# Wide products of the gate and up blocks in groups of four, the first corner's bank read out early, operands in one piece

## The chip, the cores and the metric

One core of a Trainium2 chip runs the whole program. Engines are named as in the profile: PE multiplies matrices, PEld loads its weights, DVE and ACT work on whole tiles, POOL and SP issue transfers here. The metric is the device time of one execution in microseconds (us), lower is better; three executions of the kernel before took 1763.86 to 1764.58, median 1764.16.

## The reference

Two layers; each runs three token mixers side by side, merges them, and then a feed-forward block and a gated input embedding. The change lies in the feed-forward block and in the normalisation ahead of it.

```python
for i in range(DEPTH):                      # DEPTH = 2, S = 512 tokens, D = 1024
    ...                                     # mixers, merge
    x = x + merged @ w_o[i]
    h = rmsnorm(x, norm_ffn[i])
    x = x + (jax.nn.silu(h @ w_ffn_gate[i]) * (h @ w_ffn_up[i])) @ w_ffn_down[i]   # 1024 -> 2816 -> 1024
    h = rmsnorm(x, norm_ple[i])
    x = x + jax.nn.sigmoid(h @ w_ple_gate[i]) * (p[i] @ w_ple_in[i])
```

## The kernel before

All data is float32, and every product is made of three float32r products: each operand is split into a high part and a low remainder (`split` for weights, `operand` for activations), and high x high, high x low and low x high are summed. ACT makes the high part of a weight tile, DVE the low one. Activations lie transposed, 128 channels in the partitions and 512 tokens in a row, so one PSUM bank (512 float32 in a row) holds one block of 128 outputs for all tokens.

The feed-forward block (`ffn`) goes through 22 blocks of 128 hidden units, in three parts of 8, 7 and 7, and after each part multiplies by its share of the down weights (L1141 to L1147). A block needs gate and up weights against all of h. `seven` does this with seven products in place of eight, Winograd's way on a 2x2 split: its weights are a11, a12, a22 and the sums s1 to s4 (two transfers add up weights as they land, DVE does the other sums), its activations the quarters b11, b21, b22 and their differences t1 to t4, made once for the layer in `quarters`. Each product sums over four pieces of 128 channels, for one half (256) of the tokens.

Blocks with an even number are narrow: per piece three matmuls of 256 columns (L1011 to L1013), high weights on high and low activations, then low weights on high activations. Blocks with an odd number are wide (`twice`): high and low activations stand next to each other as 512 columns, so one matmul of 512 columns (L1008) does the first two, into two halves of the bank, and one of 256 (L1009) does the third; the two halves are added afterwards on ACT and DVE. T (s1 x t3) is narrow in every block, so an odd block has six wide products.

A block uses three banks, C, A and Q, and one of the two `tr` banks for T. Even blocks take C, A, Q from the three `mm` banks, odd blocks from the two `sc` and the one `av`. C gets a11 x b11; ACT copies it to A (L1023); A gets s3 x t2, and ACT copies that to Q (L1037); C gets a12 x b21 (`corner`), which completes the gate's first half; A gets s2 x t1 and is copied out (L1043, L1044, or L1046 in a narrow block); Q gets a22 x t4 and gives the up halves; A gets s4 x b22 (L1061), which completes the gate's second half. In a wide block C and A are both read out after that last product (L1063 to L1065). The next block of the same kind can't write C before C's sum has been read, nor copy into A before A's has.

Two blocks run interleaved: `sevens_of` steps the generators, so that block n+1 does its step (a) (C and its copy), block n its (d) (s2 and a22), n+1 its (b) (T), n its (e) (s4), n+1 its (c) (s3, corner). The order on PE is that of the code. On DVE, ACT and the queues a scheduler orders by priority; the weights' loads, sums and splits run ahead with raised priority, and `behind` pins one instruction behind another on the same engine. ACT and DVE work strictly in the order that the scheduler made. The split of s3 and s4 goes into one of two fixed pairs of tiles (`spare`): `pt` for even blocks, `y` for odd ones. `held`, `mark` and `cleared` are marks for `behind`.

In the normalisation ahead of it (`w_o`, `norm_chunk`), the tile of h has its high half in columns 0 to 511 and its low half behind it. For even chunks of channels only the first 256 tokens are made, for odd ones all 512. So high and low of the same 256 tokens, the operand of a wide matmul, are two runs of 256, with a gap of 256 between them.

Of the kernel before, what the change touches and what calls it, by code (L numbers as in the profile page):

```python
# [20 lines left out]
P = 128  # L21
# [40 lines left out]
class Net:  # L62
# [212 lines left out]

    def norm_chunk(self, k, x, g, tag, st, n=512):

        if k == KD - 1:
            self.sumsq(k, x, st)
        if n < 512:  # L280
            tag = self.sb(tag, [P, 2, 512], F32R)[:, :, :n]
        h = self.operand(x[:, :n], g, tag)
        if k < KD - 1:
            self.sumsq(k, x, st)
        return h
# [675 lines left out]
    def seven(self, wg, wu, bs, tags, spare, md, first, fb, early, twice):  # L961


        nc = self.nc
        with self.tc.high_priority(offset=min(self.w_ahead, self.tc.cur_priority - self.p0)):
# [30 lines left out]
            self.tt(s4, s3, g[:, up], ALU.add)  # L996
            halve(*spare, sums[1], ("s3", "s4"))
        shape = (P, 2, 256) if twice else (P, 256)
        C, A, Q = (self.ps(t, shape) for t in tags)

        def product(out, w, b, first=False):
            wh, wl = ws[w]
            mm = nc.tensor.matmul
            for k in range(4):
                c = slice(k * P, k * P + P)
                both = bs[k][b]
                if len(out.shape) > 2:
                    mm(out, wh[:, c], both, start=first and k == 0, stop=False, skip_group_check=True)  # L1008
                    mm(out[:, 0], wl[:, c], both[:, 0], start=False, stop=k == 3, skip_group_check=True)  # L1009
                    continue  # L1010
                mm(out, wh[:, c], both[:, 0], start=first and k == 0, stop=False, skip_group_check=True)  # L1011
# [30 lines left out]
        if twice:  # L1042
            self.act(uu[:, 1], A[:, 0], AF.Copy)  # L1043
            self.cleared = self.act(gg[:, 0], A[:, 1], AF.Copy)  # L1044
        else:
            self.cleared = self.act(uu[:, 1], A, AF.Copy)  # L1046
        product(Q, "a22", "t4")
        if twice:
            self.tt(uu[:, 1], uu[:, 1], gg[:, 0], ALU.add)
            self.act(uu[:, 0], Q[:, 1], AF.Copy)  # L1050
            self.tt(uu[:, 0], Q[:, 0], uu[:, 0], ALU.add)
            self.tt(uu, uu, gg[:, 1:2].to_broadcast([P, 2, 256]), ALU.add)
        else:
# [68 lines left out]
    def ffn(self, h, x):  # L1122
# [5 lines left out]
        md8 = [self.sb(t, [P, 2, 512], F32R) for t in ["v"] * 3 + ["z"] + ["y"] * 3]  # L1128
        md8.append(tuple(self.sb("e", [P, 512], F32R) for _ in range(2)))
        self.sums, self.sevens = [t for _ in range(2) for t in self.parts_of("qk", [1024], 2)], 0  # L1130
        for part in PARTS:
            mids = md8[:len(part)]
            self.sevens_of((self.seven(self.a["w_fg"][i, fb], self.a["w_fu"][i, fb], bs,
                                       (("mm", "mm", "mm"), ("sc", "sc", "av"))[fb % 2],
                                       spare[fb % 2], md8[f], part[0] and f < 2, fb, fb == 0,
                                       fb % 2 == 1)
                            for f, fb in enumerate(part)), part[0] == 0)
# [368 lines left out]
```

## Time and profile before

| | |
|---|---|
| median of three executions | 1764.16 us (1763.86 to 1764.58) |
| the profiled execution, whole | 1764.9 us |
| its span, first to last instruction | 1763.1 us |
| granted PE clock, mean | 0.999 |
| DVE / ACT busy | 79% / 53% of the span |

The span is what the trace shows, and 1.8 us of the profiled execution lie outside it. Rows of the timeline have the start in us, the duration, the engine, the source line, and what is written from what; in square brackets stands the idle time before it and what ended it. A matmul's duration includes the way through the array, so neighbours overlap: what a matmul costs in a run of matmuls is the distance from its start to the next one's.

### The profile page before, as it was taken

Reading aid. Unit: us, or ns where it says so; the run is one execution under the profiler, and the core shown is the slowest. Engines: PE = TensorE matmul, PEld = TensorE weight load, DVE = VectorE, ACT = ScalarE, POOL = GpSimd, SP = SyncE. Lnnn points to the kernel's source line nnn. Section 1 sums busy time; section 2 is a strip of 40 time slices with the busy share of each in tenths; the row PEclk is TensorE's granted clock in tenths of the full one; section 3 lists DMA queues with packets and bytes.
Section 4 is the critical chain, followed back from the end, with each engine's and each line's share of the span. In section 5 each row is a group of like instructions: output and inputs, shape, how many; then the busy total and the mean of one; then the engine's idle time right before and its main releaser. Section 6 shows DMA issues by size and latency. Waiting matters only on the chain.

```text
span 1763.1 us, 26202 instructions
## 1 busy us (share of the span) xinstructions
PE 1756.3 (100%) x9618; PEld 1525.2 (87%) x9618; DVE 1388.2 (79%) x2264; ACT 934.6 (53%) x1649; POOL 104.1 (6%) x114
## 2 busy tenths in 40 slices
PE   9999999999999999999999999999999999999998
PEld 7889888888899898898888888888888998989987
DVE  7967988998788676777776789889887875877776
ACT  5566555326576264464545655552356653645554
POOL 0000000000121020100000000000001210201000
PEclk9999999999999999999999999999999999999999
DMA  6565641334767365543445655322356664656332
GB/s 227 163 188 157 164 123 54 102 99 150 223 161 181 119 170 154 141 118 131 149 137 166 190 148 153 111 75 93 101 182 190 180 166 122 177 143 154 97 105 96
DMA packets 114785, 253.90 MB, mean 144 GB/s; under 512 B 16864, under 2 KB 23776, under 8 KB 114656
## 3 DMA queue, kind: packets, MB, share of 16 engines
q1 hardware_dynamic: 101264, 227.83, 41.9%
q0 software_dynamic: 12672, 23.07, 8.0%
q8 instruction: 76, 1.25, 0.3%
q10 hardware_dynamic: 720, 1.31, 0.2%
q14 instruction: 53, 0.43, 0.1%
HBM read 215.46 MB, written 7.34 MB: 126 GB/s over the span
## 4 chain that ended last, share of the span: by engine, by line
PE 99%; DVE 0%; ACT 0%; POOL 0%; issue 0%; POOLq 0%; ACTq 0%; DVEq 0%
PE ffn_sc L1008 6%; PE ffn_mm L179 4%; PE ffn_mm L180 4%; PE ffn_mm L181 4%; PE ffn_mm L1011 4%; PE ffn_mm L1013 4%; PE ffn_mm L1012 4%; PE ffn_sc L1009 3%; PE mergea_mm L179 2%; PE mergea_mm L181 2%; PE mergea_mm L180 2%; PE diff_sc L798 2%; PE diff_mm L179 2%; PE diff_mm L180 2%; PE gatec_mm L180 2%; PE natten_mm L180 2%
## 5 line engine op out<-in xcount | busy, mean ns | idle before, releaser
L160 DVE SCALAR_TENSOR_TENSOR conv_z<-glu_z,pre_par,conv_z 128x512 f32<-128x512 f32 x240 | 179.4, 748 | 3.4
L143 ACT ACTIVATE ffn_wh<-ffn_wr 128x1024 fp32r<-128x1024 f32 (+1 forms) x92 | 92.6, 1020 | 117.1 <-PE ffn_mm L180 61.4
L157 DVE TENSOR_TENSOR ffn_wl<-ffn_wr,ffn_wh 128x1024 fp32r<-128x1024 f32 (+1 forms) x92 | 107.1, 1175 | 40.2 <-ACT ffn_wh L143 39.7
L976 POOL DMA_DIRECT2D ffn_qk<-w_fu x88 | 78.0, 974 | 595.6 <-DMA ffn_qk<-w_fu 308.0
L157 DVE TENSOR_TENSOR ffn_t<-ffn_mm,wo_rb 128x512 f32<-128x512 f32 (+1 forms) x86 | 47.9, 557 | 55.1 <-PE ffn_mm L181 46.9
L143 ACT ACTIVATE mergea_wh<-mergea_wr 128x1024 fp32r<-128x1024 f32 (+1 forms) x32 | 27.1, 846 | 96.8 <-PE mergea_mm L180 79.5
L157 DVE TENSOR_TENSOR ffn_t<-ffn_t,ffn_t 128x512 f32<-128x512 f32 x88 | 54.4, 619 | 18.0 <-ACT ffn_t L143 18.0
L157 DVE TENSOR_TENSOR ffn_wl<-ffn_qk,ffn_wh 128x1024 fp32r<-128x1024 f32 x44 | 53.8, 1223 | 16.6 <-ACT ffn_wh L143 16.6
L1008 PE MATMUL ffn_sc<-wo_h,ffn_wh 128*128 128x512 f32 x176 | 64.2, 399 | 0.1
L143 ACT ACTIVATE ffn_wh<-ffn_qk 128x1024 fp32r<-128x1024 f32 x44 | 46.6, 1060 | 31.4 <-PE ffn_mm L180 16.2
L143 ACT ACTIVATE diff_a<-diff_sc,diff_s 128x512 f32<-128x512 f32 x32 | 22.1, 689 | 70.8 <-DVE diff_s L891 70.8
L181 PE MATMUL ffn_mm<-ffn_v,ffn_wl 128*128 128x512 f32 x132 | 51.4, 390 | 0.0
L180 PE MATMUL ffn_mm<-ffn_v,ffn_wh 128*128 128x512 f32 x132 | 51.4, 390 | 0.0
L179 PE MATMUL ffn_mm<-ffn_v,ffn_wh 128*128 128x512 f32 x132 | 51.3, 389 | 0.0
L179 PE MATMUL ffn_mm<-ffn_y,ffn_wh 128*128 128x512 f32 x132 | 51.3, 389 | 0.0
L180 PE MATMUL ffn_mm<-ffn_y,ffn_wh 128*128 128x512 f32 x132 | 51.3, 389 | 0.0
L181 PE MATMUL ffn_mm<-ffn_y,ffn_wl 128*128 128x512 f32 x132 | 51.3, 389 | 0.0
L1011 PE MATMUL ffn_mm<-wo_h,ffn_wh 128*128 128x256 f32 x176 | 50.0, 284 | 0.0
L1012 PE MATMUL ffn_mm<-wo_h,ffn_wh 128*128 128x256 f32 x176 | 49.8, 283 | 0.0
L1013 PE MATMUL ffn_mm<-wo_h,ffn_wl 128*128 128x256 f32 x176 | 49.8, 283 | 0.0
L1009 PE MATMUL ffn_sc<-wo_h,ffn_wl 128*128 128x256 f32 x176 | 49.5, 281 | 0.0
L143 ACT ACTIVATE natten_wh<-natten_wr 128x1024 fp32r<-128x1024 f32 x24 | 25.4, 1058 | 42.1 <-issue 15.2
(847 smaller groups left out, 6325.4 us busy)
## 6 DMA issues: line engine op xcount, KB each, us to landing
ffn_qk<-w_fu POOLq DMA_DIRECT2D x88, 256.0 KB, 6.3
ffn_wr<-w_fg SPq DMA_DIRECT2D x44, 512.0 KB, 4.4
ffn_wr<-w_fd SPq DMA_DIRECT2D x32, 448.0 KB, 4.0
ffn_r<-w_fu SPq DMA_DIRECT2D x44, 256.0 KB, 3.3
ffn_qk<-w_fg SPq DMA_DIRECT2D x44, 256.0 KB, 3.2
ffn_qk<-w_fu SPq DMA_DIRECT2D x44, 256.0 KB, 3.4
natten_wr<-w_in SPq DMA_DIRECT2D x16, 512.0 KB, 4.0
diff_wr<-w_in SPq DMA_DIRECT2D x16, 512.0 KB, 4.2
```

The costliest lines, as they stand in the source:

```text
L143: i = self.nc.scalar.activation(out, in_, func, **kw)
L157: return self.nc.vector.tensor_tensor(out, a, b, op)
L160: return self.nc.vector.scalar_tensor_tensor(out, a, s, b, op0, op1)
L179: mm(out, wh, ah, start=first, stop=False, **kw)
L180: mm(out, wh, al, start=False, stop=False, **kw)
L181: mm(out, wl, ah, start=False, stop=last, **kw)
L976: nc.gpsimd.dma_start(q, wu[:, lo], accum_op=ALU.add)
L1008: mm(out, wh[:, c], both, start=first and k == 0, stop=False, skip_group_check=True)
L1009: mm(out[:, 0], wl[:, c], both[:, 0], start=False, stop=k == 3, skip_group_check=True)
L1011: mm(out, wh[:, c], both[:, 0], start=first and k == 0, stop=False, skip_group_check=True)
L1012: mm(out, wh[:, c], both[:, 1], start=False, stop=False, skip_group_check=True)
L1013: mm(out, wl[:, c], both[:, 0], start=False, stop=k == 3, skip_group_check=True)
```

## The change

Four things are edited.

1. In a wide product the four matmuls of 512 columns come first, one for each piece, and then the four of 256 columns; before they took turns.
2. In a wide block, the corner's sum is read out of C right behind the corner's product (an ACT copy of the second half, a DVE add of the first) into `gg[:, 0]`. What was parked in `gg` until then (T's copy and half of A's) goes to a tile of its own, `side`, of which there are two, taken from tag `e`.
3. A's last sum is noted in `late`, and the DVE half of the split of s3 and s4 of the next block of the same kind is pinned behind it.
4. The tile of h is laid out as [token half, high or low, 256], so that a wide matmul's 512 columns are one run. ACT and DVE write odd chunks through a pattern of 2 x 256 for this.

```diff
+        if parts:
+            x2 = x.rearrange("p (a b) -> p a b", a=2)[:, :parts]
+            h = self.operand(x2, g, tuple(tag[:, :parts, n] for n in range(2)))
...
-            h.append(self.norm_chunk(m, xo, self.par(self.i, "ffn", m), "h", st, 512 if m % 2 else 256))
+            h.append(self.sb("h", [P, 2, 2, 256], F32R))
+            self.norm_chunk(m, xo, self.par(self.i, "ffn", m), h[m], st, m % 2 + 1)
...
-        return dict(b11=ha, b21=hb[:, :, one], b22=hb[:, :, two],
+        return dict(b11=ha[:, 0], b21=hb[:, 0], b22=hb[:, 1],
...
-            halve(*spare, sums[1], ("s3", "s4"))
+            i = halve(*spare, sums[1], ("s3", "s4"))
+            if self.late[fb % 2] is not None:
+                self.behind(i, self.late[fb % 2])
+                self.late[fb % 2] = None
...
-                if len(out.shape) > 2:
-                    mm(out, wh[:, c], both, start=first and k == 0, stop=False, skip_group_check=True)
-                    mm(out[:, 0], wl[:, c], both[:, 0], start=False, stop=k == 3, skip_group_check=True)
-                    continue
+            if len(out.shape) > 2:
+                for k, c in enumerate(cols):
+                    mm(out, wh[:, c], bs[k][b], start=first and k == 0, stop=False,
+                       skip_group_check=True)
+                for k, c in enumerate(cols):
+                    mm(out[:, 0], wl[:, c], bs[k][b][:, 0], start=False, stop=k == 3,
+                       skip_group_check=True)
...
             product(C, "a12", "b21")
-            if not early and not twice:
+            if twice:
+                self.act(gg[:, 0], C[:, 1], AF.Copy)
+                self.tt(gg[:, 0], C[:, 0], gg[:, 0], ALU.add)
+            elif not early:
                 self.tt(gg[:, 0], C, self.halved(0), ALU.mult)
...
-        shared = gg[:, 1] if twice else uu[:, 0]
+        shared = side[:, 0] if twice else uu[:, 0]
...
-            self.cleared = self.act(gg[:, 0], A[:, 1], AF.Copy)
+            self.cleared = self.act(side[:, 1], A[:, 1], AF.Copy)
...
-            for n, o in enumerate((C, A)):
-                self.act(gg[:, n], o[:, 1], AF.Copy)
-                self.tt(gg[:, n], o[:, 0], gg[:, n], ALU.add)
+            self.act(gg[:, 1], A[:, 1], AF.Copy)
+            self.late[fb % 2] = self.tt(gg[:, 1], A[:, 0], gg[:, 1], ALU.add)
```

The counts of instructions are the same on every engine; on POOL and SP the order is too. What moves is shown at three places of the first layer. PE first: a11 x b11 of block 1, the first wide product; `wo_h` are the activations, `ffn_wh` and `ffn_wl` the high and low weights. Before:

```order
L1008 MATMUL ffn_sc_4911<-wo_h_4415,ffn_wh_4895 128x512
L1009 MATMUL ffn_sc_4911<-wo_h_4415,ffn_wl_4896 128x256
L1008 MATMUL ffn_sc_4911<-wo_h_4462,ffn_wh_4895 128x512
L1009 MATMUL ffn_sc_4911<-wo_h_4462,ffn_wl_4896 128x256
L1008 MATMUL ffn_sc_4911<-wo_h_4562,ffn_wh_4895 128x512
L1009 MATMUL ffn_sc_4911<-wo_h_4562,ffn_wl_4896 128x256
L1008 MATMUL ffn_sc_4911<-wo_h_4665,ffn_wh_4895 128x512
L1009 MATMUL ffn_sc_4911<-wo_h_4665,ffn_wl_4896 128x256
```

The same product in the changed kernel, whose line numbers and buffer numbers differ:

```order
L1013 MATMUL ffn_sc_4913<-wo_h_4415,ffn_wh_4897 128x512
L1013 MATMUL ffn_sc_4913<-wo_h_4462,ffn_wh_4897 128x512
L1013 MATMUL ffn_sc_4913<-wo_h_4562,ffn_wh_4897 128x512
L1013 MATMUL ffn_sc_4913<-wo_h_4665,ffn_wh_4897 128x512
L1016 MATMUL ffn_sc_4913<-wo_h_4415,ffn_wl_4898 128x256
L1016 MATMUL ffn_sc_4913<-wo_h_4462,ffn_wl_4898 128x256
L1016 MATMUL ffn_sc_4913<-wo_h_4562,ffn_wl_4898 128x256
L1016 MATMUL ffn_sc_4913<-wo_h_4665,ffn_wl_4898 128x256
```

The same eight matmuls now stand four and four, and the high weights have their last reader three matmuls earlier. DVE next, while block 1 does its middle steps and block 2 starts: `ffn_v` is block 0's result, `ffn_qk` the sums s3 and s4, `ffn_wl` block 3's first weights, `ffn_a` its a22, `ffn_pt` the low part of block 2's s3 and s4. Before:

```order
L157 TENSOR_TENSOR ffn_v_4770<-ffn_t_4808,ffn_v_4770 128x512
L157 TENSOR_TENSOR ffn_qk_4780<-ffn_qk_4780,ffn_r_4998 128x512
L157 TENSOR_TENSOR ffn_qk_4780<-ffn_qk_4780,ffn_wr_4997 128x512
L157 TENSOR_TENSOR ffn_wl_5127<-ffn_wr_5118,ffn_wh_5126 128x1024
L157 TENSOR_TENSOR ffn_t_4915<-ffn_t_4915,ffn_t_4914 128x256
L157 TENSOR_TENSOR ffn_pt_4767<-ffn_qk_4780,ffn_pt_4766 128x1024
L157 TENSOR_TENSOR ffn_a_5131<-ffn_r_5119,ffn_kh_5130 128x512
```

And now:

```order
L157 TENSOR_TENSOR ffn_v_4770<-ffn_t_4810,ffn_v_4770 128x512
L157 TENSOR_TENSOR ffn_qk_4782<-ffn_qk_4782,ffn_r_5002 128x512
L157 TENSOR_TENSOR ffn_t_4916<-ffn_sc_4913,ffn_t_4916 128x256
L157 TENSOR_TENSOR ffn_qk_4782<-ffn_qk_4782,ffn_wr_5001 128x512
L157 TENSOR_TENSOR ffn_wl_5129<-ffn_wr_5120,ffn_wh_5128 128x1024
L157 TENSOR_TENSOR ffn_a_5133<-ffn_r_5121,ffn_kh_5132 128x512
L157 TENSOR_TENSOR ffn_pt_4767<-ffn_qk_4782,ffn_pt_4766 128x1024
L157 TENSOR_TENSOR ffn_t_4917<-ffn_t_4917,ffn_e_4780 128x256
```

C's sum (`ffn_t<-ffn_sc`) has come in, a22's low part stands ahead of block 2's `ffn_pt`, and a small sum has gone behind it. On ACT the copy of C stands ahead of the copy that starts A in block 2, and the split of a22 (`ffn_kh`) ahead of that of `ffn_pt`. The third place is DVE again, some six instructions on, where block 1 is read out for the last time: `ffn_y` is the low part of block 3's s3 and s4, `ffn_sc_4911` is C and `ffn_sc_4912` is A. Before:

```order
L157 TENSOR_TENSOR ffn_t_4914<-ffn_sc_4911,ffn_t_4914 128x256
L157 TENSOR_TENSOR ffn_y_4769<-ffn_qk_4780,ffn_y_4768 128x1024
L157 TENSOR_TENSOR ffn_wl_5135<-ffn_qk_4779,ffn_wh_5134 128x1024
L157 TENSOR_TENSOR ffn_t_4914<-ffn_sc_4912,ffn_t_4914 128x256
L157 TENSOR_TENSOR ffn_t_5024<-ffn_mm_5021,wo_rb_4929 128x256
L157 TENSOR_TENSOR ffn_t_4914<-ffn_t_4914,wo_rb_4929 128x512
```

And now, where `ffn_sc_4914` is A:

```order
L157 TENSOR_TENSOR ffn_t_4916<-ffn_sc_4914,ffn_t_4916 128x256
L157 TENSOR_TENSOR ffn_t_4916<-ffn_t_4916,wo_rb_4931 128x512
L157 TENSOR_TENSOR ffn_y_4769<-ffn_qk_4782,ffn_y_4768 128x1024
L157 TENSOR_TENSOR ffn_wl_5137<-ffn_qk_4781,ffn_wh_5136 128x1024
L157 TENSOR_TENSOR ffn_t_4916<-ffn_t_4916,ffn_t_4917 128x512
L157 TENSOR_TENSOR ffn_t_5028<-ffn_mm_5025,wo_rb_4931 128x256
```

A's sum now stands ahead of two long splits, where it stood behind them.

More of the change, by code (lines that the diff above doesn't have):

```diff
@@ L274, in halves, with norm_chunk @@
         return h if isinstance(h, tuple) else (h[:, 0, :], h[:, 1, :])
-    def norm_chunk(self, k, x, g, tag, st, n=512):
+    def norm_chunk(self, k, x, g, tag, st, parts=0):
         if k == KD - 1:
             self.sumsq(k, x, st)
-        if n < 512:
-            tag = self.sb(tag, [P, 2, 512], F32R)[:, :, :n]
-        h = self.operand(x[:, :n], g, tag)
+        if parts:
+            x2 = x.rearrange("p (a b) -> p a b", a=2)[:, :parts]
+            h = self.operand(x2, g, tuple(tag[:, :parts, n] for n in range(2)))
+        else:
+            h = self.operand(x, g, tag)
         if k < KD - 1:
@@ L957, in quarters, with seven @@
         ha, hb = h[2 * j], h[2 * j + 1]
-        return dict(b11=ha, b21=hb[:, :, one], b22=hb[:, :, two],
+        return dict(b11=ha[:, 0], b21=hb[:, 0], b22=hb[:, 1],
                     **{f"t{n + 1}": o for n, o in enumerate(d)})
-    def seven(self, wg, wu, bs, tags, spare, md, first, fb, early, twice):
+    def seven(self, wg, wu, bs, tags, spare, side, md, first, fb, early, twice):
         nc = self.nc
@@ L1003, in product @@
             mm = nc.tensor.matmul
-            for k in range(4):
-                c = slice(k * P, k * P + P)
+            cols = [slice(k * P, k * P + P) for k in range(4)]
+            if len(out.shape) > 2:
[5 more added lines that the diff above has]
+                       skip_group_check=True)
+            for k, c in enumerate(cols if len(out.shape) == 2 else ()):
                 both = bs[k][b]
-                if len(out.shape) > 2:
-                    mm(out, wh[:, c], both, start=first and k == 0, stop=False, skip_group_check=True)
-                    mm(out[:, 0], wl[:, c], both[:, 0], start=False, stop=k == 3, skip_group_check=True)
-                    continue
                 mm(out, wh[:, c], both[:, 0], start=first and k == 0, stop=False, skip_group_check=True)
@@ L1048, in seven @@
         if twice:
-            self.tt(uu[:, 1], uu[:, 1], gg[:, 0], ALU.add)
+            self.tt(uu[:, 1], uu[:, 1], side[:, 1], ALU.add)
             self.act(uu[:, 0], Q[:, 1], AF.Copy)
             self.tt(uu[:, 0], Q[:, 0], uu[:, 0], ALU.add)
-            self.tt(uu, uu, gg[:, 1:2].to_broadcast([P, 2, 256]), ALU.add)
+            self.tt(uu, uu, side[:, 0:1].to_broadcast([P, 2, 256]), ALU.add)
         else:
@@ L1129, in ffn @@
         md8.append(tuple(self.sb("e", [P, 512], F32R) for _ in range(2)))
+        side = [self.sb("e", [P, 2, 256]) for _ in range(2)]
+        self.late = [None, None]
         self.sums, self.sevens = [t for _ in range(2) for t in self.parts_of("qk", [1024], 2)], 0
@@ L1134, in ffn @@
                                        (("mm", "mm", "mm"), ("sc", "sc", "av"))[fb % 2],
-                                       spare[fb % 2], md8[f], part[0] and f < 2, fb, fb == 0,
-                                       fb % 2 == 1)
+                                       spare[fb % 2], side[fb % 2], md8[f], part[0] and f < 2,
+                                       fb, fb == 0, fb % 2 == 1)
                             for f, fb in enumerate(part)), part[0] == 0)
```

## The prediction

> **What bounds it.** I read the page first, for which engine ends last, then the chain that ended last, then the table of waits for PE alone, and then PE's own rows in the feed-forward block.
>
> ```profile
> PE 1756.3 (100%) x9618; PEld 1525.2 (87%) x9618; DVE 1388.2 (79%) x2264; ACT 934.6 (53%) x1649; POOL 104.1 (6%) x114
> PE 99%; DVE 0%; ACT 0%; POOL 0%; issue 0%; POOLq 0%; ACTq 0%; DVEq 0%
> PE pre_av L329 <- DVE pre_zeror L402: 1.1, 1, 1.1
> ```
>
> PE is busy all the time, the chain is PE from end to end, and the only wait that the table knows is the 1.1 us ahead of the first matmul. So only two things can change the time: the distances between matmuls' starts, and waits so short that the overlapping durations hide them in that table. DVE and ACT matter only where PE comes to wait for them. Both have to be read from starts. First the distances, in stretches of one kind: block 1's s3 and a12 products (wide and narrow matmuls in turn), block 2's a11 (narrow only), and a stretch of the down product (512 columns only).
>
> ```profile
> 504.88 0.39 PE L1008 MATMUL ffn_sc<-wo_rp,ffn_y 128*128 128x512 f32 x1
> ...
> 506.29 0.40 PE L1008 MATMUL ffn_sc<-wo_h,ffn_wh 128*128 128x512 f32 x1
> ...
> 507.70 0.28 PE L1011 MATMUL ffn_mm<-wo_h,ffn_wh 128*128 128x256 f32 x1
> ...
> 509.14 0.40 PE L1008 MATMUL ffn_sc<-wo_rp,ffn_wh 128*128 128x512 f32 x1
> ```
> ```profile
> 599.70 0.39 PE L180 MATMUL ffn_mm<-ffn_v,ffn_wh 128*128 128x512 f32 x1
> ...
> 605.59 0.39 PE L179 MATMUL ffn_mm<-ffn_v,ffn_wh 128*128 128x512 f32 x1
> ```
>
> From 504.88 to 507.70 there are eight pairs, 352.5 ns each. From 507.70 to 509.14 there are twelve narrow matmuls, 120 ns each. From 599.70 to 605.59 there are 26 steps, 226.5 ns each. A wide and a narrow matmul among their own kind would take 346.5, so taking turns costs 6 ns a pair.
>
> **Grouping.** The counts come from the whole span, by line:
>
> ```profile
> 0.00:1763.10 1763.10, 189.75 (x528) 99.42 (x528) 1.00 0.51 144
> ```
>
> L1008 has 528 matmuls, which is 132 wide products of four (11 odd blocks, six products, two layers). If every pair saves 6 ns, a product saves 24 ns. A grouped product keeps one passage from narrow to wide and one back, where it had four of each; if they cost what they do now, three quarters remain, 18 ns. I take 20, nearer to the lower end since the passages stay: 132 x 20 ns = **2.6 us**, from 132 x 18 = 2.4 to 132 x 24 = 3.2 us; below nothing only if a group of like matmuls were slower than the same matmuls in turn, and the two stretches of one kind exclude that.
>
> **One piece.** The s3 product reads its activations in one run (wo_rp), the a12 product in two (wo_h, an h tile). They take 506.29 - 504.88 = 1.41 and 507.70 - 506.29 = 1.41 us. I cost this part at nothing; ACT and DVE write the same elements to other addresses, with PE's first use of the last chunk after them:
>
> ```profile
> 491.39 0.75 DVE L160 SCALAR_TENSOR_TENSOR wo_h<-wo_x,pre_par,wo_h 128x512 fp32r<-128x512 f32 x1
> ...
> 493.53 0.28 PE L1011 MATMUL ffn_tr<-wo_h,ffn_pt 128*128 128x256 f32 x1
> ```
>
> It ends at 492.14 and is used at 493.53; without those 1.39 us of cover, a slower pattern would show by its excess, once a layer. The Trainium skill, page Advanced Engine Details and Errata, section PSUM Cachelines, says that an access pattern with gaps slows a matmul much, and by it this part should pay on the half of the products that read h. The equal 1.41 us speak against it for runs of 256, and the sum stays.
>
> **Short waits that go.** Around block 3's start PE leaves its step of 0.12 twice.
>
> ```profile
> 517.29 0.42 DVE L157 TENSOR_TENSOR ffn_t<-ffn_sc,ffn_t 128x256 f32<-128x256 f32 x1
> ...
> 517.55 0.28 PE L1013 MATMUL ffn_mm<-wo_h,ffn_wl 128*128 128x256 f32 x1
> ...
> 517.86 0.47 PE L1008 MATMUL ffn_sc<-wo_h,ffn_wh 128*128 128x512 f32 x1
> ...
> 518.16 0.28 PE L1009 MATMUL ffn_sc<-wo_h,ffn_wl 128*128 128x256 f32 x1
> ...
> 519.04 1.22 DVE L157 TENSOR_TENSOR ffn_wl<-ffn_qk,ffn_wh 128x1024 fp32r<-128x1024 f32 x1
> ...
> 521.82 0.58 ACT L143 ACTIVATE ffn_sc<-ffn_sc 128x512 f32<-128x512 f32 x1
> ...
> 523.38 0.36 ACT L143 ACTIVATE ffn_t<-ffn_mm 128x256 f32<-128x256 f32 x1
> ...
> 523.50 0.28 PE L1013 MATMUL ffn_tr<-wo_z,ffn_wl 128*128 128x256 f32 x1
> ...
> 523.79 0.39 PE L1011 MATMUL ffn_mm<-wo_h,ffn_pt 128*128 128x256 f32 x1
> ...
> 524.01 0.28 PE L1012 MATMUL ffn_mm<-wo_h,ffn_pt 128*128 128x256 f32 x1
> ```
>
> At 517.86 block 3's first matmul starts 0.15 after DVE has read block 1's C (517.29 + 0.42 = 517.71). The step before it is 0.31 instead of 0.12 and the next 0.30 instead of 0.235: 0.26 us lost. With C read behind the corner this goes. At 523.79 block 2's s4 product waits for ACT's copy of A, which ended at 523.74; that copy stood behind the one that starts block 3's A, which could not run before DVE had read block 1's A, two long splits late. Steps of 0.29 and 0.22 instead of 0.12: 0.27 us. With A's sum ahead of the splits this goes too. The second layer shows the same two starts:
>
> ```profile
> 1391.10 0.47 PE L1008 MATMUL ffn_sc<-wo_h,ffn_wh 128*128 128x512 f32 x1
> ...
> 1397.00 0.39 PE L1011 MATMUL ffn_mm<-wo_h,ffn_pt 128*128 128x256 f32 x1
> ```
>
> Together 2 x 0.53 = **1.06 us**.
>
> **What is late next.** The moved ACT copy waits for the corner's product; queued behind it on ACT are the copy that starts block 2's A and the next weight splits. The moved DVE sum has the sum s4, block 3's weights, a22's low part and then `ffn_pt` behind it, and PE waits for `ffn_pt` in block 2's s3 product. The tightest place of the trace is that one:
>
> ```profile
> 507.78 1.06 ACT L143 ACTIVATE ffn_wh<-ffn_qk 128x1024 fp32r<-128x1024 f32 x1 [0.17 <-PE ffn_sc L1008]
> ...
> 508.87 1.23 DVE L157 TENSOR_TENSOR ffn_wl<-ffn_qk,ffn_wh 128x1024 fp32r<-128x1024 f32 x1 [0.54 <-ACT ffn_wh L143]
> ...
> 510.62 0.68 DVE L157 TENSOR_TENSOR ffn_qk<-ffn_qk,ffn_r 128x512 f32<-128x512 f32 x1
> 511.34 0.69 DVE L157 TENSOR_TENSOR ffn_qk<-ffn_qk,ffn_wr 128x512 f32<-128x512 f32 x1
> 511.95 1.22 DVE L157 TENSOR_TENSOR ffn_wl<-ffn_wr,ffn_wh 128x1024 fp32r<-128x1024 f32 x1
> 513.08 0.42 DVE L157 TENSOR_TENSOR ffn_t<-ffn_t,ffn_t 128x256 f32<-128x256 f32 x1
> 513.42 1.22 DVE L157 TENSOR_TENSOR ffn_pt<-ffn_qk,ffn_pt 128x1024 fp32r<-128x1024 f32 x1
> 514.55 0.68 DVE L157 TENSOR_TENSOR ffn_a<-ffn_r,ffn_kh 128x512 fp32r<-128x512 f32 x1
> ...
> 515.03 0.29 PE L1013 MATMUL ffn_mm<-wo_rp,ffn_pt 128*128 128x256 f32 x1
> ...
> 515.15 0.69 DVE L157 TENSOR_TENSOR ffn_qk<-ffn_qk,ffn_r 128x512 f32<-128x512 f32 x1
> ```
>
> `ffn_pt` ends at 514.64, and PE needs it at 515.03, a margin of 0.39. By steps from start to start: C's sum adds 0.34, less the 0.12 by which the s4 sum now waits for s3 anyway (0.72 instead of 0.60); a22's low part, now ahead, adds 0.60; the small sum that goes behind takes 0.34 away. That is 0.48 later. Against it, the chain begins earlier: ACT's split at 507.78 waits for the last wide matmul of the corner, which starts at about 506.29 + 3 x 0.227 = 506.97 instead of 507.35; ACT is then busy until about 507.5, so some 0.28 is won. `ffn_pt` would end at 514.84 and release PE at 514.99 (0.15 as at 517.86). PE, six grouped products further on by 0.12, comes at 514.91: 0.08 of waiting and 0.10 for the slow step behind a wait, as at 523.79. I take **0.2 us a layer, 0.4 in all**; from nothing (0.1 more won) to 0.46 a layer, 0.9 in all, if the early start isn't won.
>
> The pin behind A's sum (`late`) lets two small instructions, that sum and the scaling behind it, at most 0.42 + 0.68 us, pass the two splits, and makes the splits wait for ACT's copy of A, made over a microsecond before. `ffn_wl`, the later split, ended at 519.04 + 1.22 = 520.26 and would end by 521.4; its user, block 3's T, starts eleven steps of 0.12 before 523.50, at 522.2. I cost the pin at nothing, and at the excess over that 0.8 if the cover is gone.
>
> **Sum.** 2.6 + 1.06 - 0.4 = 3.3 us: 1764.9 becomes 1761.6 for an execution like the profiled one. That one was 0.74 above the median, so the median should be 1764.16 - 3.3 = **1760.9 us**. By the bounds: 3.2 + 1.06 = 4.3 gives 1759.9, and 2.4 + 1.06 - 0.9 = 2.6 gives 1761.6.
>
> **Rivals.** *Waits only move* (0.15): DVE's longer queue costs as much as the two waits, 1764.16 - 2.6 = 1761.6. For it: the margin of 0.39 is smaller than the 0.48 added. Against: the early start.
>
> *Grouping pays nothing* (0.13): the 6 ns belong to something else than the turns, such as two matmuls that share activations now standing apart. Then 1.06 - 0.4 = 0.7 remains, 1763.5. [...]
>
> *ACT's copies come late in every even block* (0.05), slower than before. In the steady blocks the same copy of A has little room:
>
> ```profile
> 541.05 1.06 ACT L143 ACTIVATE ffn_wh<-ffn_wr 128x1024 fp32r<-128x1024 f32 x1 [0.55 <-PE ffn_mm L1012]
> ...
> 543.06 0.36 ACT L143 ACTIVATE ffn_t<-ffn_mm 128x256 f32<-128x256 f32 x1
> ...
> 543.82 0.28 PE L1011 MATMUL ffn_mm<-wo_h,ffn_pt 128*128 128x256 f32 x1
> ```
>
> It ends at 543.42, 0.40 ahead of its user. If the moved copy and sum (0.36 and 0.42) pushed it by 0.78, each of 20 even blocks would lose 0.38 + 0.10, 9.6 us; less 2.6 + 1.06, the time would be 1770.1. It decides from a delay of 0.40. Against it: ACT stood idle for 0.55 at 541.05, waiting for PE, and that swallows what comes earlier; the work on ACT and DVE is the same in sum.
>
> *More than the sum* (0.05): the wide matmuls get faster than any in the trace; below 1759.9.
>
> **Chances.** The forecast has 0.62. About 0.2%, 3.5 us, is what a measurement of this kernel can tell from no change, so faster means below 1760.6. The forecast lies 0.3 us short of that, and I give 0.33 of its 0.62 to faster; with the last rival 0.38. Slower is 0.05, the rest, 0.57, is the same. The range runs from 1759.6 to 1763.3: it takes in the bounds, the first rival and the near part of the second, and leaves out the third and the fourth.
>
> **What would show it.** In the changed profile a wide product should take 1.39 us and not 1.41, with starts of four wide matmuls 0.227 apart; the starts at block 3's first product and at block 2's s4 product should have even steps; block 2's s3 product may show one step of 0.2 to 0.3 at its third matmul. Wide steps still near 0.236 inside a group would refute the largest term; steps over 0.2 in later even blocks would mean the slow rival.

## The result, and the profile after

The changed kernel takes **1761.60 us** (median of 22 runs, 1761.12 to 1762.58); beside it the kernel before takes 1764.43 us (22 runs, 1763.67 to 1765.18). The ratio is 0.9984, 95% interval 0.9978 to 0.9990: a gain of 2.8 us, 0.16%, which is no chance result and yet inside the 0.2% that was to count as the same. The profiled executions are 1764.9 us before and 1761.63 us after, 3.3 us apart.

The page after still has PE busy all the time, and the chain of work that ended last is PE alone:

```profile
span 1759.9 us, 26200 instructions
...
PE 1753.2 (100%) x9618; PEld 1524.8 (87%) x9618; DVE 1389.9 (79%) x2264; ACT 930.5 (53%) x1649; POOL 104.0 (6%) x114
...
PE 99%; DVE 0%; ACT 0%; POOL 0%; issue 0%; POOLq 0%; ACTq 0%; DVEq 0%
```

So the gain has to be read from starts again. The timeline of PE, after, over block 1's s3 and a12 products (neighbours of one form are put together, xN; the start is that of the first):

```profile
504.81 0.62 PE L1013 MATMUL ffn_sc<-wo_rp,ffn_y 128*128 128x512 f32 x2
505.27 0.62 PE L1013 MATMUL ffn_sc<-wo_z,ffn_y 128*128 128x512 f32 x2
505.73 0.40 PE L1016 MATMUL ffn_sc<-wo_rp,ffn_y 128*128 128x256 f32 x2
505.96 0.40 PE L1016 MATMUL ffn_sc<-wo_z,ffn_y 128*128 128x256 f32 x2
506.20 1.08 PE L1013 MATMUL ffn_sc<-wo_h,ffn_wh 128*128 128x512 f32 x4
507.13 0.64 PE L1016 MATMUL ffn_sc<-wo_h,ffn_wl 128*128 128x256 f32 x4
507.61 0.28 PE L1020 MATMUL ffn_mm<-wo_h,ffn_wh 128*128 128x256 f32 x1
```

The two products take 507.61 - 504.81 = 2.80 us, where they took 2.82: 1.39 for s3 and 1.41 for a12. Four wide starts take 0.92 to 0.93 us, so a wide step inside a group is 0.232 and not 0.227. Over all rows of both layers (each distance from a product's matmul to the next start, in us):

| steps of the gate and up products | before | after | difference |
|---|---|---|---|
| 512 columns (528) | 124.26 | 122.41 | -1.85 |
| the 256 columns that belong to them (528) | 62.15 | 62.45 | +0.30 |
| narrow products and T (2112) | 253.44 | 252.15 | -1.29 |
| sum | 439.84 | 437.00 | -2.84 |

Of the -2.84, 1.06 are the two waits a layer that are gone (0.14 among the wide steps, 0.92 among the narrow ones). The other 1.78 us are the grouping, 1.78 / 132 = 13.5 ns a product. Outside these rows the two profiled executions differ by some 0.4 us, nearly all of it in the two layers' stages of one mixer, which the change doesn't touch; 2.84 is also the distance of the medians.

The places where PE waited before, block 3's first product and block 2's s4 product, in the timeline after:

```profile
517.41 0.28 PE L1022 MATMUL ffn_mm<-wo_h,ffn_wl 128*128 128x256 f32 x1
517.53 1.09 PE L1013 MATMUL ffn_sc<-wo_h,ffn_wh 128*128 128x512 f32 x4
518.46 0.51 PE L1016 MATMUL ffn_sc<-wo_h,ffn_wl 128*128 128x256 f32 x3
...
522.45 0.36 ACT L143 ACTIVATE ffn_t<-ffn_mm 128x256 f32<-128x256 f32 x1
...
523.08 0.28 PE L1022 MATMUL ffn_tr<-wo_z,ffn_wl 128*128 128x256 f32 x1
523.21 0.28 PE L1020 MATMUL ffn_mm<-wo_h,ffn_pt 128*128 128x256 f32 x1
```

Both have even steps: 517.53 comes 0.12 after its neighbour, 523.21 comes 0.13 after, with ACT's copy done at 522.81, 0.40 ahead.

And the place where a new wait was forecast, block 2's s3 product:

```profile
507.42 1.05 ACT L143 ACTIVATE ffn_wh<-ffn_qk 128x1024 fp32r<-128x1024 f32 x1
...
508.50 1.23 DVE L157 TENSOR_TENSOR ffn_wl<-ffn_qk,ffn_wh 128x1024 fp32r<-128x1024 f32 x1 [0.25 <-ACT ffn_wh L143]
...
510.85 0.42 DVE L157 TENSOR_TENSOR ffn_t<-ffn_sc,ffn_t 128x256 f32<-128x256 f32 x1
511.18 0.68 DVE L157 TENSOR_TENSOR ffn_qk<-ffn_qk,ffn_wr 128x512 f32<-128x512 f32 x1
...
513.52 1.22 DVE L157 TENSOR_TENSOR ffn_pt<-ffn_qk,ffn_pt 128x1024 fp32r<-128x1024 f32 x1
...
514.77 0.28 PE L1021 MATMUL ffn_mm<-wo_rp,ffn_pt 128*128 128x256 f32 x1
514.89 0.28 PE L1022 MATMUL ffn_mm<-wo_rp,ffn_pt 128*128 128x256 f32 x1
515.01 0.28 PE L1020 MATMUL ffn_mm<-wo_rp,ffn_pt 128*128 128x256 f32 x1
```

C's sum stands in the queue as the order said, `ffn_pt` ends at 514.74, and PE takes its third matmul at 514.89 in step. There is no wait.

### The profile page after: what moved, and what is told of

It reads as the page before. It is cut to its first block, busy times and chain, and to the rows that moved or that the text cites. A ratio compares the mean times of both kernels' runs of the same rounds, so it can differ in the third digit from the quotient of the medians.

```text
span 1759.9 us, 26200 instructions
## 1 busy us (share of the span) xinstructions
PE 1753.2 (100%) x9618; PEld 1524.8 (87%) x9618; DVE 1389.9 (79%) x2264; ACT 930.5 (53%) x1649; POOL 104.0 (6%) x114
## 4 chain that ended last, share of the span: by engine, by line
PE 99%; DVE 0%; ACT 0%; POOL 0%; issue 0%; POOLq 0%; ACTq 0%; DVEq 0%
PE ffn_sc L1013 6%; PE ffn_mm L179 4%; PE ffn_mm L180 4%; PE ffn_mm L181 4%; PE ffn_mm L1020 4%; PE ffn_mm L1022 4%; PE ffn_mm L1021 4%; PE ffn_sc L1016 3%; PE mergea_mm L181 2%; PE mergea_mm L179 2%; PE mergea_mm L180 2%; PE diff_sc L800 2%; PE diff_mm L180 2%; PE diff_mm L179 2%; PE natten_mm L180 2%; PE gatec_mm L180 2%
## 5 line engine op out<-in xcount | busy, mean ns | idle before, releaser
L1013 PE MATMUL ffn_sc<-wo_h,ffn_wh 128*128 128x512 f32 x176 | 48.0, 394 | 0.0
L893 DVE TENSOR_REDUCE diff_s<-diff_sc 128x1 f32<-128x512 f32 x64 | 42.1, 682 | 2.2 <-PE diff_sc L800 2.2
L157 DVE TENSOR_TENSOR ffn_t<-ffn_t,ffn_t 128x512 f32<-128x512 f32 x44 | 30.2, 687 | 16.9 <-ACT ffn_t L143 16.8
```

What stands on the lines that cost most here:

```text
L157: return self.nc.vector.tensor_tensor(out, a, b, op)
L1013: mm(out, wh[:, c], bs[k][b], start=first and k == 0, stop=False, skip_group_check=True)
```

## The experiments

Eight kernels ran. e1 to e4 were measured beside 33 runs of the kernel before (median 1764.67 us), e5 to e8 beside 21 (1764.77 us). "Steps" are the sum of the table above.

**e1: before, with the grouping alone**

```diff
+            if len(out.shape) > 2:
+                for k, c in enumerate(cols):
+                    mm(out, wh[:, c], bs[k][b], start=first and k == 0, stop=False, ...)
+                for k, c in enumerate(cols):
+                    mm(out[:, 0], wl[:, c], bs[k][b][:, 0], start=False, stop=k == 3, ...)
-                if len(out.shape) > 2:
-                    mm(out, wh[:, c], both, ...)
-                    mm(out[:, 0], wl[:, c], both[:, 0], ...)
-                    continue
```

> The kernel before with the grouping of the wide products alone. Theory (passages between sizes cost time, and the waits belong to the other edits): a wide product takes about 1400 ns in place of 1411, as in the changed profile, the narrow matmuls behind it lose a few ns, together 13 to 14 ns a product or 1.8 us; the two waits of each layer at block 3's first product and block 2's s4 product stay, 0.5 us a layer. Time 1.8 us below before. Rival (the 3.3 us of span that the changed profile gained are mostly waits): no more than 1 us below. Rival (one run of 512 columns is needed for the gain): the wide matmuls with operands in two runs (a11, a12, s4) keep 235 ns while those of s3, s2 and a22 get shorter.

Measured: 1762.73 us, ratio 0.9990 (0.9981 to 0.9999); steps 438.10. The theory had the two waits of each layer stay where they were, and that fell: at block 3 and at block 2's s4 product they are all but gone (one step of 0.270 is left at 517.9), and one has come up at block 5's first product, in both layers. DVE and PE of e1 there:

```profile
537.61 0.75 DVE L157 TENSOR_TENSOR ffn_t<-ffn_sc,ffn_t 128x256 f32<-128x256 f32 x2
...
537.62 0.28 PE L1016 MATMUL ffn_mm<-wo_h,ffn_wl 128*128 128x256 f32 x1
538.17 0.93 PE L1007 MATMUL ffn_sc<-wo_h,ffn_wh 128*128 128x512 f32 x3 [0.27 <-DVE ffn_t L157]
```

DVE reads the two banks one behind the other; the first reading ends near 537.61 + 0.42 = 538.03, and PE starts 0.14 later, 0.55 after the matmul ahead of it instead of 0.12. The next step is 0.306. With the 0.04 at 517.9 that is 0.54 us a layer, 1.08 in all, as much as before; without it the steps are 438.10 - 1.08 = 437.02, the changed kernel's number. So the wait for the bank belongs to the late reading of C and moves where the order puts it, and the grouping alone is worth 1.8 us.

The order that the scheduler makes on DVE has changed too, though only the order on PE was edited. Where block 1 is read out for the last time, A's sum (519.12) stands between the two long splits; before it stood behind both:

```profile
517.98 1.23 DVE L157 TENSOR_TENSOR ffn_y<-ffn_qk,ffn_y 128x1024 fp32r<-128x1024 f32 x1 [0.31 <-ACT ffn_y L143]
519.12 0.42 DVE L157 TENSOR_TENSOR ffn_t<-ffn_sc,ffn_t 128x256 f32<-128x256 f32 x1
519.46 1.22 DVE L157 TENSOR_TENSOR ffn_wl<-ffn_qk,ffn_wh 128x1024 fp32r<-128x1024 f32 x1
```

With that the wait at block 2's s4 product is gone without the early reading and without the pin.

**e2: before, with the early reading of C, `side` and the pin, without the grouping**

```diff
+            if twice:
+                self.act(gg[:, 0], C[:, 1], AF.Copy)
+                self.tt(gg[:, 0], C[:, 0], gg[:, 0], ALU.add)
...
-            for n, o in enumerate((C, A)):
-                self.act(gg[:, n], o[:, 1], AF.Copy)
-                self.tt(gg[:, n], o[:, 0], gg[:, n], ALU.add)
+            self.act(gg[:, 1], A[:, 1], AF.Copy)
+            self.late[fb % 2] = self.tt(gg[:, 1], A[:, 0], gg[:, 1], ALU.add)
```

> The kernel before with the early reading of C, the side tile and the pin behind A's sum, but wide and narrow matmuls in turn and the old layout of h. Theory: the two waits go (1.06 us for two layers), but without the grouping the high weights of the corner are released 0.35 us later, so that the low part of block 2's s3 and s4 ends at about 515.05 instead of 514.73 and PE waits for it: one step of 0.25 to 0.35 us at the third matmul of block 2's s3 product and a slow one behind it, about 0.25 us a layer. Time 0.4 to 0.7 us below before. Rival (this wait was never near): both waits gone and no new one, 1.06 us below. Rival (waits only move): no difference from before.

Measured: 1763.86 us, ratio 0.9997 (0.9988 to 1.0006), which by itself is no difference; steps 439.43, 0.41 below before, as the theory had it. The two old waits are gone in both layers, and here the forecast new one is there. ACT, DVE and PE of e2:

```profile
507.57 1.06 ACT L143 ACTIVATE ffn_wh<-ffn_qk 128x1024 fp32r<-128x1024 f32 x1 [0.17 <-PE ffn_sc L1011]
...
508.67 1.23 DVE L157 TENSOR_TENSOR ffn_wl<-ffn_qk,ffn_wh 128x1024 fp32r<-128x1024 f32 x1 [0.54 <-ACT ffn_wh L143]
...
513.68 1.22 DVE L157 TENSOR_TENSOR ffn_pt<-ffn_qk,ffn_pt 128x1024 fp32r<-128x1024 f32 x1
...
514.70 0.28 PE L1015 MATMUL ffn_mm<-wo_rp,ffn_pt 128*128 128x256 f32 x1
...
514.95 0.19 PEld L1016 LDWEIGHTS ffn_mm<-wo_rp,ffn_pt 128*128 128x128 f32 x1 [0.18 <-DVE ffn_pt L157]
514.96 0.39 PE L1016 MATMUL ffn_mm<-wo_rp,ffn_pt 128*128 128x256 f32 x1
515.18 0.28 PE L1014 MATMUL ffn_mm<-wo_rp,ffn_pt 128*128 128x256 f32 x1
```

`ffn_pt` ends at 514.90, where PE would have started at 514.82. The steps are 0.26 and 0.22 instead of 0.12, 0.24 us a layer. The chain begins with ACT's split at 507.57, which waits for the corner's last wide matmul; in the changed kernel the split waits for nothing. The traces are shifted against each other as a whole, so the start of DVE's part is best counted from PE's start of block 1's s3 product: 4.00 us here (504.67 to 508.67), 3.99 before, 3.69 in the changed kernel (504.81 to 508.50) and 3.70 in e1. So the early reading brings the wait, and the grouping takes it away. One more step of 0.325 at 533.3 costs 0.09 a layer; its cause was not followed. Without both the steps are 439.43 - 0.66 = 438.77; the kernel before without its waits has 439.84 - 1.06 = 438.78. By the steps, nothing else changed.

**e3: before, with the new layout of h alone** (`norm_chunk` and `quarters` as in the change)

```diff
-        return dict(b11=ha, b21=hb[:, :, one], b22=hb[:, :, two],
+        return dict(b11=ha[:, 0], b21=hb[:, 0], b22=hb[:, 1],
```

> The kernel before with the new layout of h alone (a wide matmul's 512 columns in one run). Theory: nothing, within 0.3 us of before, and wide steps of 235 ns for a11, a12 and s4 as before. Rival (gaps in a pattern slow a matmul): these three products, half of all wide ones, get shorter; at 8 ns for each wide matmul that would be 264 x 8 ns = 2.1 us.

Measured: 1764.44 us, ratio 0.9998 (0.9990 to 1.0007); steps 439.84, as before, with the mean wide step at 235.1 ns in both. The layout does nothing, neither on PE nor where h is written. The rule of the Trainium skill (page Advanced Engine Details and Errata, section PSUM Cachelines) that gaps slow a matmul does not show for an operand in two runs of 256; the section's heading speaks of PSUM, and may not mean operands at all.

**e4: the change without the pin**

```diff
-            if self.late[fb % 2] is not None:
-                self.behind(i, self.late[fb % 2])
-                self.late[fb % 2] = None
```

> The changed kernel without the pin of the split of s3 and s4 behind A's sum. Theory: the pin is what removes the second wait, since without it the long splits stand ahead of A's sum on DVE as before; so the wait at block 2's s4 product comes back, 0.27 us a layer, 0.5 us in all, while the one at block 3's first product stays gone. Rival (the early reading of C alone is enough): no wait comes back and the time is that of the changed kernel within 0.3 us.

Measured: 1761.66 us, ratio 0.9984 (0.9975 to 0.9993); steps 437.00, and no wait comes back. My theory, that the pin keeps the second wait away, fell. DVE of e4 where block 1 is read out for the last time:

```profile
517.13 0.42 DVE L157 TENSOR_TENSOR ffn_t<-ffn_sc,ffn_t 128x256 f32<-128x256 f32 x1
517.59 0.69 DVE L157 TENSOR_TENSOR ffn_t<-ffn_t,wo_rb 128x512 f32<-128x512 f32 x1
518.19 1.22 DVE L157 TENSOR_TENSOR ffn_y<-ffn_qk,ffn_y 128x1024 fp32r<-128x1024 f32 x1
519.33 1.22 DVE L157 TENSOR_TENSOR ffn_wl<-ffn_qk,ffn_wh 128x1024 fp32r<-128x1024 f32 x1
```

A's sum (517.13) stands ahead of both splits without any pin. The pin changes the order only in later odd blocks, where `ffn_y` would stand ahead of A's sum, and there nobody waits for it.

**e5: the change in groups of two** (two wide, two narrow, two wide, two narrow)

```diff
-                for k, c in enumerate(cols):
-                    mm(out, wh[:, c], bs[k][b], ...)
-                for k, c in enumerate(cols):
-                    mm(out[:, 0], wl[:, c], bs[k][b][:, 0], ...)
+                for ks in ((0, 1), (2, 3)):
+                    for k in ks:
+                        mm(out, wh[:, cols[k]], bs[k][b], ...)
+                    for k in ks:
+                        mm(out[:, 0], wl[:, cols[k]], bs[k][b][:, 0], ...)
```

> The changed kernel with groups of two: two wide, two narrow, two wide, two narrow in each wide product. Theory (each passage narrow to wide and back costs some time, and the group's length does not matter otherwise): four passages a product gave 1411 ns, one gave 1400, so two give about 1404, and the kernel is 0.5 to 0.8 us above the changed one. Rival (what pays is only that wide follows wide): three of four wide matmuls followed a wide one in the changed kernel, two of four here, so about 1404 too, but with the steps of 233 and 236 in every group of two, not the later 228 and 232. Rival (the gain comes from waits): the time of the changed kernel.

Measured: 1761.44 us, ratio 0.9983 (0.9974 to 0.9992), the changed kernel's time and not 0.5 to 0.8 us more. The steps are 437.17, of which 0.34 are the wait at `ffn_pt` (0.17 a layer: `ffn_pt` ends at 515.36, PE would start at 515.35; counted as in e2, DVE starts 3.86 us on, so the chain has won less than half of what the fours win); without it 436.83. PE of e5 in block 1's a12 product:

```profile
506.67 0.62 PE L1014 MATMUL ffn_sc<-wo_h,ffn_wh 128*128 128x512 f32 x2
507.13 0.40 PE L1017 MATMUL ffn_sc<-wo_h,ffn_wl 128*128 128x256 f32 x2
507.36 0.63 PE L1014 MATMUL ffn_sc<-wo_h,ffn_wh 128*128 128x512 f32 x2
```

Half the product takes 507.36 - 506.67 = 0.69 us. The theory that each passage between sizes has a fixed price, so that twos keep half of the cost, fell. The rival that forecast this time, that the gain comes from waits, is excluded by the steps without waits, here and in e1.

**e6: the change with two products' wide matmuls together** (s3 with a12, s2 with a22: eight wide, then eight narrow)

```diff
+        if twice:
+            product(A, "s3", "t2", part=(0,))
+            product(C, "a12", "b21", part=(0,))
-        product(A, "s3", "t2")
+        product(A, "s3", "t2", part=(1,))
...
-            product(C, "a12", "b21")
+            product(C, "a12", "b21", part=(1,))
```

> The changed kernel with two products of a step merged: eight wide matmuls (s3 and a12, then s2 and a22), then their eight narrow ones. Theory (passages, with a tail of some matmuls behind each): two passages fewer in each wide block, 44 in all, at 11 to 14 ns each 0.5 to 0.6 us below the changed kernel, and the last four of the eight wide matmuls at 226 to 229 ns, near the 226.5 of a long run. Rival (in this block a wide matmul takes 232 whatever stands around it, by its operands or by other traffic): the eight stay at 232 on average, and the time is that of the changed kernel. Rival (slower): the sums are read out up to 0.9 us later, and a copy or split that had 0.4 us of room makes PE wait, 0.1 to 0.5 us in each pair of blocks, 2 to 10 us in all.

Measured: 1767.98 us, ratio 1.0019 (1.0010 to 1.0028), slower than before. PE waits in ten places, five in each layer, for 3.2 us a layer. The longest is at `ffn_pt` of block 2; DVE and PE of e6:

```profile
515.04 1.22 DVE L157 TENSOR_TENSOR ffn_pt<-ffn_qk,ffn_pt 128x1024 fp32r<-128x1024 f32 x1
...
515.22 0.28 PE L1023 MATMUL ffn_mm<-wo_rp,ffn_pt 128*128 128x256 f32 x1
516.31 0.39 PE L1024 MATMUL ffn_mm<-wo_rp,ffn_pt 128*128 128x256 f32 x1 [0.81 <-DVE ffn_pt L157]
```

A product that is finished later hands on its result later, and here that reaches PE. Without the waits the steps are 443.35 - 6.4 = 436.95. The mean wide steps by place in a run of eight, those that waited left out, are 233.0, 234.9, 229.8, 231.7, 231.2, 230.0, 226.3 and 230.5 ns. Two kinds of run stand behind the last three: those of s3 and a12 come down to 227.3, 226.7 and 226.8, as the theory had it, those of s2 and a22 do not (232.8, 226.0 and 234.2). In sum longer groups bring nothing more.

**e7: the change with the third matmul 512 columns wide too.** This adds low x low to the wide products, so the output has one small term more, and no two sizes meet inside a product.

```diff
-                    mm(out[:, 0], wl[:, c], bs[k][b][:, 0], start=False, stop=k == 3,
+                    mm(out, wl[:, c], bs[k][b], start=False, stop=k == 3,
```

> The changed kernel with the third matmul of each piece also 512 columns wide, which adds the product of the two low parts: a wide product is then eight matmuls of 512 columns and no size changes inside it. Theory (passages): after the first two or three they settle at 226 to 227 ns, a product takes about 1820 ns, and the whole is 132 x 0.42 = 55 us longer than the changed kernel. Rival (232 belongs to this block's operands or traffic): 232 throughout, 1856 ns a product, 60 us longer.

Measured, in one execution: 1819.23 us, 57.6 above the changed kernel. The mean of the 1056 wide steps is 229.6 ns, between the theory's and the rival's. PE of e7 in block 1's a12 product, behind eight wide matmuls of s3:

```profile
507.07 1.07 PE L1013 MATMUL ffn_sc<-wo_h,ffn_wh 128*128 128x512 f32 x4
507.98 1.07 PE L1016 MATMUL ffn_sc<-wo_h,ffn_wl 128*128 128x512 f32 x4
508.89 0.28 PE L1020 MATMUL ffn_mm<-wo_h,ffn_wh 128*128 128x256 f32 x1
```

The eight steps take 508.89 - 507.07 = 1.82 us, 227.5 ns each. Behind a narrow matmul the steps begin at 232.6, 235.6, 228.7, 232.3, 230.9 and are down at 226.7 to 226.9 from the sixth. In the runs of s3 and a12 they stay at 226.6 to 226.7 from the seventh to the sixteenth, across the change of product. In those of s2 and a22 they stay down to the ninth and rise again from a22's second matmul on (233.3, 225.8, 235.9); why was not found. And block 15's first product, which comes behind a down product of 512 columns, has 226.5 to 227 from its first matmul on, in this kernel as in the changed one. So it is the change of size ahead that makes the first steps long, as the theory said, and not this block's operands; it takes five matmuls to settle and not two or three, and a22 is a disturbance that neither theory has.

**e8: the change with all blocks wide but the first of each layer**

```diff
-                                       fb, fb == 0, fb % 2 == 1)
+                                       fb, fb == 0, fb > 0)
```

> The changed kernel with every block wide but the first of each layer. A narrow product takes twelve matmuls of 120 ns, 1440; a wide one 1400: 20 blocks more, six products, 40 ns each, are 4.8 us below the changed kernel if nothing waits. Theory: DVE does 1.4 us and ACT 1.5 us more in each of these blocks, where DVE was busy for 84 to 94% of the time, so PE waits for splits and the kernel is slower than the changed one, by up to 20 x 1 us. Rival (DVE has room enough): 3 to 5 us faster.

Measured: **1757.29 us** (5 runs, 1756.94 to 1757.65), ratio 0.9959 (0.9947 to 0.9972) to the kernel before, and the intervals of this ratio and the changed kernel's do not meet. The early reading and the pin come along in these blocks, since both hang on `twice`. Ten more blocks in each of two layers turn 120 narrow products of 12 x 0.120 = 1.44 us into wide ones of 1.40. PE of e8 in block 2's s3 product:

```profile
514.18 0.62 PE L1013 MATMUL ffn_mm<-wo_rp,ffn_pt 128*128 128x512 f32 x2
514.64 0.62 PE L1013 MATMUL ffn_mm<-wo_z,ffn_pt 128*128 128x512 f32 x2
515.11 0.40 PE L1016 MATMUL ffn_mm<-wo_rp,ffn_pt 128*128 128x256 f32 x2
515.34 0.40 PE L1016 MATMUL ffn_mm<-wo_z,ffn_pt 128*128 128x256 f32 x2
515.58 1.09 PE L1013 MATMUL ffn_mm<-wo_h,ffn_wh 128*128 128x512 f32 x4
```

From 514.18 to 515.58 it takes 1.40 us. The estimate was 120 x 0.04 = 4.8 us; the steps fall from 437.00 to 432.72, 4.3 us, and the median by 4.3. My theory here, that ACT and DVE could not carry the additional reading out, fell. Busy time in the stretch from 505 to 557 us, first the changed kernel and then e8 (us of 52 for each engine):

```profile
sum 52.00, PE 52.00 PEld 49.04 DVE 46.44 ACT 36.01 POOL 9.24; mean PE 52.00 PEld 49.04 DVE 46.44 ACT 36.01 POOL 9.24
```

```profile
sum 52.00, PE 52.00 PEld 46.38 DVE 48.05 ACT 40.62 POOL 8.81; mean PE 52.00 PEld 46.38 DVE 48.05 ACT 40.62 POOL 8.81
```

ACT has 4.6 us more to do and DVE 1.6, of 52, and both stay below the span. PE has no long step in the gate and up products that the changed kernel doesn't have too.

## Why the prediction was right, and where it was not

The forecast was 1760.9 us, within 0.2% of before; 1761.60 came out, in the range. Of the 0.7 between them, 0.27 is the kernel before, whose median is 1764.43 with 22 executions and was 1764.16 with three. The sum of 3.3 us was 2.8, and its terms came out so:

| term | forecast, us | measured, us | shown by |
|---|---|---|---|
| grouping | -2.6 (2.4 to 3.2) | -1.8 | e1, and the steps |
| one piece | 0 | 0 | e3 |
| two short waits a layer | -1.06 | -1.06 | starts at 517.53 and 523.21; e2 |
| new wait at `ffn_pt` | +0.4 (0 to 0.9) | 0 | starts at 514.77 to 515.01 |
| pin | 0 | 0 | e4 |

Two errors of opposite sign, 0.8 us too much for the grouping and 0.4 for a wait that did not come, leave the sum as near as it is; that is partly luck.

**Grouping: the mechanism holds, the size was off.** The rival that grouping pays nothing fell with e1. It was mis-sized in the step "if they cost what they do now, three quarters remain, 18 ns", and the bounds, which stopped at 18, were too narrow: 13.5 ns came out. That step gave every passage between sizes the same price and every other wide matmul the 226.5 ns of the down product. Neither holds. The mean wide steps by place in a group of four behind narrow matmuls are 233.6, 233.9, 229.8 and 230.4 ns, and what is saved doesn't go with the number of passages:

| order inside a product (steps without waits) | us | saved, ns a product |
|---|---|---|
| in turn (before) | 438.78 | |
| twos (e5) | 436.83 | 14.8 |
| fours (the change) | 437.00 | 13.5 |
| eights over two products (e6) | 436.95 | 13.9 |

Strict turns cost something and pairs already give all of it back. By e7, about five wide matmuls must go ahead before a step comes down to 226.7 ns, and a group of four ends before that. The shape is not the same in every kernel: in e8 the mean steps by place are 230.2, 230.8, 235.0 and 229.0. What makes the first ones long was not found out.

The Trainium skill, page TensorE: Matmul & The Clock Gate, section Back-to-back issue gap, gives columns / 2.4 + 2.5 ns as the gap of an isolated matmul, and says itself that a stream of weight loads and matmuls departs from it; neither it nor its figures for a stream have a term for what stands beside a matmul. By that e1 and e5 would have gained nothing from the grouping; they show 1.8 and 1.95 us, so here the measurement decides against it.

**The two short waits** were rightly read from starts, 0.26 and 0.27 a layer, and both went. What the prediction says of the reasons is shown for the first: without the early reading (e1) the wait for C's bank comes back at another block. For the second the runs agree with the reason, but no single edit can be named for it: the wait is gone in e1 (grouping alone), in e2 (without the grouping) and in e4 (without the pin), and in each of them A's sum stands ahead of at least one of the two splits. The early reading alone, without grouping and pin, was not run. The prediction's chain also lacks a link. Before, DVE had read A at 520.60 (520.18 + 0.42), but the ACT copy that starts block 3's A began only at 521.82, behind a weight split that waited for PE:

```profile
520.86 1.06 ACT L143 ACTIVATE ffn_wh<-ffn_wr 128x1024 fp32r<-128x1024 f32 x1 [1.77 <-PE ffn_mm L1012]
```

After, that copy stands ahead of the split and starts at 519.18. So before, the copy was late by its place on ACT and not by DVE's sum alone; that a late sum is what puts it there was not tested.

**The new wait did not come**, and the step that failed is "releases PE at 514.99 (0.15 as at 517.86)". That 0.15 was the distance from DVE's last reading of a PSUM bank to the matmul that overwrites it. For a weight tile it is 0.05: e2 ends `ffn_pt` at 514.90 and loads it at 514.95. (The other wait of the trace before shows 0.05 as well, from the end of ACT's copy at 523.74 to 523.79.) With 0.05, even the forecast end of 514.84 would have let PE go at 514.89, ahead of the 514.91 at which it was to come.

The rest of that forecast was near. The trace after is ahead by 0.07 as a whole at this place (block 1's s3 product starts at 504.81 and not at 504.88). With 0.07 put back, the chain began 0.30 earlier than before, where 0.28 was forecast; `ffn_pt` ended at 514.81, forecast 514.84; and PE came at 514.96 and not at 514.91, since the grouping saved less. That smaller saving made room as well. e2 shows that the wait hangs on the early start too: without the grouping it is there at 0.24 a layer. For an early start that isn't won the prediction had 0.46; 0.10 less by the distance and 0.12 less because PE is not brought forward is 0.24.

The other rivals: "waits only move" gave nearly the measured time, 1761.6, and is still wrong, since no wait came in place of the two (e1 and e2, each without a part of the change, are the cases in which one does). "More than the sum" did not happen: the wide steps are 231.8 ns on average, not below the 226.5 of the trace before, and 1761.60 lies above 1759.9. "ACT's copies come late" did not happen: no wait of that kind appears. The profiled executions are 3.3 us apart, which is the sum that was forecast, but by chance: 0.8 us too much for the grouping are made up by the 0.4 of the wait that did not come and 0.4 that belong to another stage.

## What to carry to other kernels

Where PE is never idle by the table of waits, read the distances between starts: they showed 1.06 us of waits that no table lists, and a cost of turns that is taken away by the order alone, for which groups of two are enough. A neighbouring edit can pay for a wait that another edit makes (here the grouping frees a weight tile three matmuls earlier), so measure each alone and together before dropping one. And try the obvious larger dose of what works: making nearly all blocks wide was worth 4.3 us, more than the whole change, though DVE looked too busy for it.

## What the runs showed of the hardware

- PE goes on 0.05 us after DVE's last write of a weight tile (514.90 to 514.95 in e2; 516.26 to 516.31 in e6; 515.36 to 515.41 in e5) and after ACT's last reading of a PSUM bank to which it then adds (523.74 to 523.79 before; 568.93 to 568.98 in e6), but 0.14 to 0.15 us after DVE's last reading of a PSUM bank that it is to overwrite (538.03 to 538.17 in e1; 517.71 to 517.86 before). Whether the reading engine or the overwriting makes the difference was not tested.
- The matmul that waited takes a longer step itself: 0.22 instead of 0.12 at 256 columns (before, e2, e5, e6), and 0.305 to 0.34 instead of 0.235 at 512 (before, e1, e6). So a short wait costs 0.07 to 0.10 us more than its length.
- Matmuls of 512 and 256 columns in strict turns take 352.5 ns a pair. In groups of two or four a pair takes 14.8 / 4 = 3.7 or 13.5 / 4 = 3.4 ns less, counting what the narrow products around them gain (0.7 of the 3.4), and longer groups bring no more.
- Behind a narrow matmul, wide ones start at 230 to 236 ns and are down at 226.7 to 226.9 from the sixth (e7); behind the 512 columns of a down product they take 226.5 to 227 from the first (block 15 of e7 and of the changed kernel). a22 of e7 is an exception without a known reason.
